# First down projection of a decoder layer in products of 512 columns, with the S5 setup cut in two and moved

## The chip, the cores and the metric

The kernel runs on one core of one Trainium2 chip. The metric is the device time of one execution in microseconds (us). Five engines work side by side, each through its own instructions in order: TensorE (PE, matrix products; its weight loads are listed as PEld), VectorE (DVE), ScalarE (ACT), GpSimd (POOL) and SyncE (SP, which here issues nearly all DMA transfers).

## The reference

One layer of a decoder trunk in float32, for 1024 tokens of width 1024 and a feed-forward width of 2816:

```
h = rms_norm(x, norm_w[0]);  x = x + 0.5 * (silu(h @ gate) * (h @ up)) @ down
h = rms_norm(x, norm_w[1]);  p = h @ w_in
y_A = S5(u)      lr = min(lam_re, -1e-4); dt = exp(log_dt); a = exp(lr*dt) * (cos(li*dt) + i sin(li*dt))
                 f = (a - 1)/(lr + i li);  Bb = f * B;  scan x_t = a x_{t-1} + Bb u_t;  y = Re(C x_t) + D u
y_B = HGRN2(q, f, v, g);   y_C = RG-LRU(conv(xb), gate)
x = x + (sum_b sigmoid(gate_b) * (y_b @ branch_proj_b)) @ w_out
h = rms_norm(x, norm_w[2]);  x = x + 0.5 * (second SwiGLU of h)
return rms_norm(x, final_norm_w)
```

S5 has 32 groups of 16 channels with 64 complex states each. What depends on its weights alone (powers of a, the products with B and C, a table of rotations) is computed in the kernel, and this setup is what the change moves.

## The kernel before

Every float32 operand of a product is split into two parts, high (h, a copy on ACT, L156 or L219) and low (l, the difference, on DVE, L157 or L220). A product of two split operands is three matmuls into the same PSUM bank (`mm3`, lines L207 to L209): wh with ah, wl with ah, wh with al. In the trace a matmul reads `ps<-w,ah`: first the moving operand with its columns, then the stationary one, a block of 128x128 that a weight load brings in ahead of it.

The first feed-forward has three stages. **Gate-up** (`gate_up`) makes the 22 blocks of silu(gate)*up by a scheme with seven products in place of eight (`tile7`). The **first down** (`down`, L526) multiplies blocks 0 to 9 of that result, the chunks CH1 = (4, 6), with the down weights. The other twelve blocks follow in `down7`, again by sevens. In `down` the results stand in four tiles X of 128 x 2 x 1024. A product covers 256 output columns (cq) and two row tiles (e) that share one PSUM bank of 512 columns, so that a matmul has 256 moving columns:

```
for e in range(2):
    t0 = (g % 2) * 256 + e * P
    ...
    self.mm3(ps[:, e * 256:(e + 1) * 256], pairs)
nc.vector.scalar_tensor_tensor(out=x, in0=ps.rearrange("p (e c) -> p e c", e=2), scalar=0.5, in1=x, op0=ALU.mult, op1=ALU.add)
next(hooks, None)
```

The last call but one (L558) is the evacuation: DVE adds half of the bank to x. Products of kind "g" have four banks, so the fifth product waits for the evacuation of the first. `next_units` hands out split weights from a ring of slots (RB = 3 raw tiles, HB = 6 halves); `a_split` loads and splits the blocks of the gate-up result (ar, ah, al).

`hooks` is the generator `s5_prep` (L1164): each product runs it to its next `yield`. It computes, in this order, the small values (tiles s5w, ex, An, half, tbc: 16 to 32 columns each, several hundred DVE instructions), Bb from B and those values, a table of rotations in four batches (tiles oc, os, otm; every other batch on POOL), and then eight batches of sums and turns. The sums of a batch are BA (two products and their sum) and Cn (the same, 576 columns). The second product of each, btm and t, runs on POOL, and DVE adds it. The turns are eight transposes on PE (L1372, ident or swap with BA), four products of Cn with Bb (L1383), and copies of their results.

A scheduler, not the order of the code, fixes each engine's order when the kernel is built: it places an instruction when its inputs should be there by its own costs, and `high_priority(PRIO)` moves splits ahead. On the chip each engine then keeps that fixed order.

Later, `s5_glu` and the merge of the three branches follow the mixers, and the second feed-forward ends with `down7` again, for which AL = 7 is the depth of the buffers `al`.

Of the kernel before, what the change touches and what calls it, by code (L numbers as in the profile page):

```python
# [12 lines left out]
P = 128  # L13
# [48 lines left out]
class Trunk:  # L62
    PRIO = 400
    RB, HB = 3, 6
# [188 lines left out]
    def x_in(self, g, cq):  # L253
        return self.I["x"][g * 256:(g + 1) * 256, cq * 256:(cq + 1) * 256].rearrange("(i p) c -> p i c", p=P)
# [93 lines left out]
    def ffn_units(self, n, chunks):  # L348
        g, u, dn = self.I["ffn_gate"][0, n], self.I["ffn_up"][0, n], self.I["ffn_down"][0, n]
        for f in range(NFF):  # L350
            self.add_cols(g, f * P, kind="n" if f < self.STD else "g")
            self.add_cols(u, f * P, kind=("n", "v")[f] if f < self.STD else "u")
        f0 = 0
        for c in chunks:
            step = c if c <= 4 else c // 2
            for cq in range(4):
                for f in range(f0, f0 + c, step):
                    self.add_cols(dn, cq * 256, f, step, 256)
            f0 += c
        self.d_units(n, f0 // 2)  # L360
# [141 lines left out]
    def a_load(self, upto, tag):  # L502
        while self.n_al < min(upto, len(self.aq)):
# [7 lines left out]
            self.nc.sync.dma_start(out=t, in_=self.abuf[f, hf])  # L511
# [14 lines left out]
    def down(self, chunks, x_src, hooks):  # L526
# [5 lines left out]
        for ci, c in enumerate(chunks):  # L532
            nu = 1 if c <= 4 else 2
# [4 lines left out]
            step = 2 if ci == 0 else 1  # L538
            for cq0 in range(0, 4, step):
                ws = {}  # L540
                for g, cq in ((2 * hf + i, cq0 + q) for hf in range(2) for q in range(step) for i in range(2)):
                    if cq not in ws:
                        ws[cq] = self.next_units(nu)
                    w = ws[cq]
                    x = self.X[g][:, :, cq * 256:(cq + 1) * 256]
# [3 lines left out]
                    for e in range(2):  # L549
                        t0 = (g % 2) * 256 + e * P  # L550
                        pairs = []
                        for k in range(c):
                            a = self.a[f0 + k, g // 2]
                            wt = w[k * nu // c]
                            kk = k % (c // nu)
                            pairs.append(((a[0][:, t0:t0 + P], a[1][:, t0:t0 + P]), (wt[0][:, kk, :], wt[1][:, kk, :])))
                        self.mm3(ps[:, e * 256:(e + 1) * 256], pairs)
                    nc.vector.scalar_tensor_tensor(out=x, in0=ps.rearrange("p (e c) -> p e c", e=2), scalar=0.5, in1=x, op0=ALU.mult, op1=ALU.add)  # L558
                    next(hooks, None)
                    if cq == 3 and g == 1 and ci > 0:  # L560
                        self.a_split(n1 + after)
                if cq0 + step == 4:
# [581 lines left out]
class S5(Mixer):  # L1144

    L = 8
# [4 lines left out]
    def s5_setup(self):  # L1151
        for _ in self.s5_prep():
            pass

# [9 lines left out]
    def s5_prep(self):  # L1164
        nc = self.nc
        V, A, G = nc.vector, nc.scalar, nc.gpsimd
        c = self.const
        NG, L, GB, NK = self.NG, self.L, self.GB, self.NK
        tt = lambda o, a, b, op, e=V: e.tensor_tensor(out=o, in0=a, in1=b, op=op)
        M, AD, SU = ALU.mult, ALU.add, ALU.subtract  # L1170
# [6 lines left out]

        self.rho = c.tile([P, NG], F32, name="rho")
        self.sc_w = [self.dram(n, (P, NG, P)) for n in ("s5w1a", "s5w1b", "s5ca1", "s5ca2")]
        self.sc_t = [self.dram(n, (P // 2, NG, NK)) for n in ("s5tc", "s5ts")]  # L1180
# [3 lines left out]
        swap = self.slot("p", (P, P), name="swap")  # L1184
        V.tensor_copy(swap[:, 0:64], self.ident[:, 64:128])
        V.tensor_copy(swap[:, 64:128], self.ident[:, 0:64])

        w = self.slot("p", (P, 16, NG), name="s5w")
        pr = self.slot("p", (P, 3, NG), name="s5p")
        self.get(pr, self.I["s5p"])  # L1190
        B1, B2, C1, C2 = (self.slot("p", (P, NG, 16), name=n) for n in ("B1", "B2", "C1", "C2"))
        for i, t in enumerate((B1, B2, C1, C2)):
            self.get(t, self.I["s5bc"][i])
        dsk = c.tile([16, NG], F32, name="dsk")
        self.get(dsk, self.I["s5d"])
        lr, dt, mag, th, n, cs, sn, den, f0, f1, t0, t1, fr, fi, e0, e1 = (w[:, i, :] for i in range(16))
        self.late = tsc(lr, pr[:, 0, :], -1e-4, ALU.min)
# [33 lines left out]
        tsc(fi, fi, sg, M)  # L1231

        An = [self.slot("p", (P, L + 1, NG), name=f"An{i}") for i in range(4)]
# [6 lines left out]
        tmp = self.slot("p", (P, L + 1, NG), name="tmp")  # L1240
        k = 1
        while k < L:
# [9 lines left out]
            k *= 2  # L1252
        tsc(sAr, Ar, sg, M)
# [6 lines left out]
        rv = self.slot("p", (P, 2, L, NG), name="rv")  # L1260
# [5 lines left out]
        Bb1, Bb2 = (self.slot("p", (P, NG, 16), name=n) for n in ("Bb1", "Bb2"))  # L1266
        tb = self.slot("p", (P, NG, 16), name="tb")
        frb, fib = (x.unsqueeze(2).to_broadcast([P, NG, 16]) for x in (fr, fi))
        tt(Bb1, B1, frb, M)
        tt(tb, B2, fib, M)  # L1270
        tt(Bb1, Bb1, tb, SU)
        tt(Bb2, B2, frb, M)
        tt(tb, B1, fib, M)
        tt(Bb2, Bb2, tb, AD)
        yield

        TB = 16
        HG = NG // 2
        tc_, ts_ = (self.slot("p", (P, HG, TB), name=n) for n in ("tbc", "tbs"))
# [20 lines left out]
        for _ in range(3):  # L1300
            square(er, ei, er, ei)
        er, ei, t0, t1 = (halved(t) for t in (er, ei, t0, t1))
# [3 lines left out]
        tmt = self.slot("p", (P, HG, TB // 2), name="tmt")  # L1306

        def double(oc, os, xc, xs, r, i, tm, gn, k, e=V):
            rb, ib = (x.unsqueeze(2).to_broadcast([P, gn, k]) for x in (r, i))
            tt(oc, xc, rb, M, e)  # L1310
            tt(tm, xs, ib, M, e)
            tt(oc, oc, tm, SU, e)
            tt(os, xc, ib, M, e)
            tt(tm, xs, rb, M, e)
            tt(os, os, tm, AD, e)
# [5 lines left out]
        mu = self.slot("p", (P, 6, HG), name="mu")  # L1321
        cur = (er, ei)
        for m in range(3):
            V.tensor_copy(mu[:, 2 * m, :], er)
            V.tensor_copy(mu[:, 2 * m + 1, :], ei)
            if m < 2:
                square(er, ei, er, ei)
        yield
# [17 lines left out]
        for b in range(nb):  # L1346
# [14 lines left out]
            flat = lambda t: t.rearrange("p g n c -> p g (n c)")  # L1361
# [6 lines left out]
            yield  # L1368
# [20 lines left out]
            self.put(self.sc_K[:, gs, :], kt)  # L1389
            yield  # L1390
# [86 lines left out]
class Hybrid(S5):  # L1477
# [166 lines left out]
    def ffn1(self):  # L1644
        nc = self.nc
        tiles = {}
        with ExitStack() as R:
            with ExitStack() as L:
# [25 lines left out]
                self.gate_up(0, lambda: self.t_first(normed(0, 2), 0, 2), lambda: self.t_second(normed(1), 0), self.CH1, {6: self.hg_masks, 9: self.hg_setup, 12: self.s5_zeros, 15: self.rg_setup}, 2)  # L1674
# [16 lines left out]
            self.w_open(self.H)  # L1691
# [126 lines left out]
```

## Time and profile before

| | us |
|---|---|
| median of 3 runs | 2298.42 (2298.32 to 2301.26) |
| the profiled execution, its own time | 2294.33 |
| its span, first to last instruction | 2292.1 |
| PE busy | 2238.5 |
| DVE busy | 1647.7 |
| ACT busy | 992.6 |
| POOL busy | 213.5 |

The span is 2.2 us shorter than that execution's own time, and the execution 4.1 us shorter than the median. Matmuls overlap in the pipeline, so the busy time of PE says where it had work, not how fast it went; the distance from one matmul's start to the next one's says that. A matmul that waits has in brackets how long PE stood idle before it and what is inferred to have released it.

### The profile page before, as it was taken

The page shows a single profiled execution, that of the slowest core. Times are in us where ns is not written, and L with a number is a line of the kernel's source. Part 1 is how long each engine was busy: PE and PEld are TensorE (multiplying, and loading weights), DVE is VectorE, ACT ScalarE, POOL GpSimd, SP SyncE. Part 2 cuts the span into 40 slices and gives each one's busy share as a digit, 9 for nine tenths or more (in the row PEclk, how much of TensorE's full clock was granted, in tenths as well). Part 3 has the DMA queues.
Part 4 walks back from the last instruction along what each step waited for, and adds up shares of the span by engine and source line. Part 5 has one row for each costly group of instructions (what it writes and reads, how often), then busy time and mean ns, then how long its engine had stood idle before and what let it go on. Part 6 is the DMA issues. An engine that isn't in the chain of part 4 may idle for free. (4 is left out here: it accounts for less than half of the span.)

```text
span 2292.1 us, 32136 instructions
## 1 busy us (share of the span) xinstructions
PE 2238.5 (98%) x11540; PEld 1889.0 (82%) x11540; DVE 1647.7 (72%) x2912; ACT 992.6 (43%) x1696; POOL 213.5 (9%) x218
## 2 busy tenths in 40 slices
PE   7999999999999999999999999999999999999998
PEld 6788888899789888888777788798978888888886
DVE  6876676699698765657777678867486766665797
ACT  5223222322457433435666666645432222234454
POOL 0200000004200300000000045610020000000000
PEclk9999999999999999999999999999999999999999
DMA  5122433474844465754343745356513433347633
GB/s 157 56 83 83 118 115 120 143 255 136 261 151 146 115 187 166 221 156 140 127 132 127 220 133 175 111 171 207 161 33 115 161 109 120 102 138 287 221 101 122
DMA packets 354367, 336.96 MB, mean 147 GB/s; under 512 B 44048, under 2 KB 258448, under 8 KB 354192
## 3 DMA queue, kind: packets, MB, share of 16 engines
q1 hardware_dynamic: 354208, 334.92, 46.4%
q8 instruction: 90, 1.47, 0.3%
q14 instruction: 69, 0.57, 0.1%
HBM read 233.53 MB, written 102.50 MB: 147 GB/s over the span
## 5 line engine op out<-in xcount | busy, mean ns | idle before, releaser
L207 PE MATMUL ps<-T,w 128*128 128x512 f32 (+1 forms) x992 | 380.7, 387 | 1.5 <-DVE T L309 1.2
L208 PE MATMUL ps<-T,w 128*128 128x512 f32 (+1 forms) x992 | 379.5, 384 | 1.3 <-DVE T L310 1.3
L209 PE MATMUL ps<-T,w 128*128 128x512 f32 (+1 forms) x992 | 376.3, 384 | 1.6 <-DVE w L157 1.6
L156 ACT CAST w<-raw 128x1024 fp32r<-128x1024 f32 (+2 forms) x218 | 182.2, 837 | 323.3 <-PE ps L208 290.6
L157 DVE TENSOR_TENSOR w<-raw,w 128x1024 fp32r<-128x1024 f32 (+2 forms) x218 | 216.7, 995 | 118.6 <-ACT w L156 113.6
L156 ACT CAST w<-S 128x1024 fp32r<-128x1024 f32 x128 | 134.5, 1051 | 337.1 <-PE ps L208 327.7
L208 PE MATMUL ps<-TT,w 128*128 128x512 f32 x640 | 252.3, 394 | 4.4 <-DVE TT L310 4.4
L207 PE MATMUL ps<-TT,w 128*128 128x512 f32 x640 | 250.6, 393 | 0.0
L209 PE MATMUL ps<-TT,w 128*128 128x512 f32 x640 | 249.6, 392 | 0.0
L209 PEld LDWEIGHTS ps<-T,w 128*128 128x128 f32 x992 | 187.3, 189 | 39.4 <-DVE w L157 3.1
L208 PEld LDWEIGHTS ps<-T,w 128*128 128x128 f32 x992 | 187.3, 189 | 38.5 <-DVE T L310 1.5
L207 PEld LDWEIGHTS ps<-T,w 128*128 128x128 f32 x992 | 186.4, 189 | 39.5 <-DVE T L309 1.9
L157 DVE TENSOR_TENSOR w<-S,w 128x1024 fp32r<-128x1024 f32 x128 | 158.7, 1240 | 73.3 <-ACT w L156 73.3
L411 DVE TENSOR_TENSOR g<-g,ps 128x512 f32<-128x512 f32 x132 | 90.2, 684 | 134.2 <-PE ps L209 125.7
L208 PEld LDWEIGHTS ps<-TT,w 128*128 128x128 f32 x640 | 120.8, 189 | 36.0 <-DVE TT L310 11.4
L207 PEld LDWEIGHTS ps<-TT,w 128*128 128x128 f32 x640 | 121.4, 190 | 25.7
L209 PEld LDWEIGHTS ps<-TT,w 128*128 128x128 f32 x640 | 121.1, 189 | 24.3
L156 ACT CAST ah<-ar 128x512 fp32r<-128x512 f32 (+2 forms) x153 | 80.2, 525 | 139.5 <-PE ps L208 89.4
L208 PE MATMUL ps<-b,ah 128*128 128x512 f32 x360 | 139.3, 389 | 0.0
L207 PE MATMUL ps<-b,ah 128*128 128x512 f32 x360 | 137.4, 389 | 0.0
L209 PE MATMUL ps<-b,ah 128*128 128x512 f32 x360 | 126.7, 390 | 0.0
L157 DVE TENSOR_TENSOR ah<-ar,ah 128x512 fp32r<-128x512 f32 (+2 forms) x153 | 85.8, 567 | 42.3 <-ACT ah L156 34.5
(414 smaller groups left out, 4884.3 us busy)
## 6 DMA issues: line engine op xcount, KB each, us to landing
raw<-in_w_in_dram SPq DMA_DIRECT2D x56, 512.0 KB
raw<-in_ffn_gate_dram SPq DMA_DIRECT2D x44, 512.0 KB
raw<-in_ffn_up_dram SPq DMA_DIRECT2D x44, 512.0 KB
B<-in_ffn_down_dram SPq DMA_DIRECT2D x68, 256.0 KB
ar<-s SPq DMA_DIRECT2D x68, 256.0 KB
ar<-a SPq DMA_DIRECT2D x66, 256.0 KB
s<-S SPq DMA_DIRECT2D x62, 256.0 KB
a<-a SPq DMA_DIRECT2D x56, 256.0 KB
```

What stands on the lines that cost most here:

```text
L156: self.nc.scalar.copy(hi, src)
L157: self.last_lo = self.nc.vector.tensor_tensor(out=lo, in0=src, in1=hi, op=ALU.subtract)
L207: nc.tensor.matmul(out=ps, lhsT=lh, rhs=rh, start=start and j == 0, stop=False, skip_group_check=skip)
L208: nc.tensor.matmul(out=ps, lhsT=lh, rhs=rl, start=False, stop=False, skip_group_check=skip)
L209: self.last_mm = nc.tensor.matmul(out=ps, lhsT=ll, rhs=rh, start=False, stop=stop and j == n - 1, skip_group_check=skip)
L411: tt = lambda o, a, b: nc.vector.tensor_tensor(out=o, in0=a, in1=b, op=ALU.add)
```

## The change

- **Products of 512 columns.** In `down` a product is now one row tile (q of 8) by one half of the columns, with one bank and one matmul of 512 columns per step. Weights come in units of two blocks by 512 columns, seven slots of halves (HB = 7), and x comes in sixteen loads of 128x512, issued behind the eighth load of the gate-up result.
- **Small values in gate-up.** `s5_small` is a generator of its own, run one step per gate-up block from f = 3, with its tiles in a pool of its own.
- **The rest of the setup, sums a batch ahead.** `s5_prep` starts with B and C, then Bb, the table and the sums of batch 0; after that the sums of batch b + 1 are issued before the turns of batch b.
- **Pools.** 13 slots p and 4 slots pc instead of 14 and 3; `w_open` moves to the next pool; the last down has 6 buffers al.

```
-    RB, HB = 3, 6
+    RB, HB = 3, 7
...
-            step = c if c <= 4 else c // 2
-            for cq in range(4):
-                for f in range(f0, f0 + c, step):
-                    self.add_cols(dn, cq * 256, f, step, 256)
+            for half in range(2):
+                for f in range(f0, f0 + c, 2):
+                    self.add_cols(dn, half * HALF, f, 2, HALF)
...
             if ci == 0:
+                self.a_split(2 * c)
+                first_a = self.a_ins
                 self.a_split(2 * c + sum(chunks[1:2]))
...
+            for half in range(2):
+                w = self.next_units(c // 2)
+                for q in range(8):
+                    x = self.X[q // 2][:, q % 2, half * HALF:(half + 1) * HALF]
                     if ci == 0:
-                        nc.sync.dma_start(out=x, in_=x_src(g, cq))
+                        with self.tc.issue_after(first_a.ins):
+                            nc.sync.dma_start(out=x, in_=x_src(q, half))
                     ps = self.ps("g")
...
+                    c0 = slice((q % 4) * P, (q % 4 + 1) * P)
+                    pairs = []
+                    for k in range(c):
+                        a, wt = self.a[f0 + k, q // 4], w[k // 2]
+                        pairs.append(((a[0][:, c0], a[1][:, c0]), (wt[0][:, k % 2], wt[1][:, k % 2])))
+                    self.mm3(ps, pairs)
+                    nc.vector.scalar_tensor_tensor(out=x, in0=ps, scalar=0.5, in1=x, op0=ALU.mult, op1=ALU.add)
                     next(hooks, None)
...
-        for b in range(nb):
+        def sums(b):
...
-            yield
+            return BA, Cn
+
+        def turned(b, BA, Cn):
+            gs = slice(b * GB, (b + 1) * GB)
             for q, idm in enumerate((self.ident, swap)):
...
+        last = sums(0)
+        yield
+        for b in range(nb):
+            new = sums(b + 1) if b + 1 < nb else None
+            yield
+            turned(b, *last)
+            last = new
             yield
...
+                small = self.s5_small()
+                midway = {f: lambda: next(small, None) for f in range(3, NFF)}
+                midway.update({6: self.hg_masks, 9: self.hg_setup, 12: self.s5_zeros, 15: self.rg_setup})
+                self.gate_up(0, lambda: self.t_first(normed(0, 2), 0, 2), lambda: self.t_second(normed(1), 0), self.CH1, midway, 2)
...
+            for _ in small:
+                pass
             with ExitStack() as c:
                 self.open_pool(c, a=24)
-                self.open_pool(c, "left", p=14, pt=6, pc=3)
+                self.open_pool(c, "left", p=13, pt=6, pc=4)
                 self.down(self.CH1, self.x_in, self.prep())
...
-            self.open_pool(R, al=7, X=4, fw=1)
+            self.AL = 6
+            self.open_pool(R, al=6, X=4, fw=1)
```

**DVE where the first down begins.** `al` are low parts of the gate-up result, `x<-ps` the evacuation of the first product, `ex` and `s5w` small values of S5. Before, the evacuation stands behind a run of `al` with two small instructions between each pair:

```order
586 L220 TENSOR_TENSOR al_3913<-ar_3900,ah_3912 128x512
587 L800 TENSOR_SCALAR ex_4062<-ex_4063 128x32
588 L1176 SCALAR_TENSOR_TENSOR s5w_4019<-s5w_4019 128x32
589 L220 TENSOR_TENSOR al_3919<-ar_3902,ah_3918 128x512
590 L802 SCALAR_TENSOR_TENSOR ex_4063<-ex_4062,ex_4063 128x32
591 L1176 SCALAR_TENSOR_TENSOR s5w_4019<-s5w_4019 128x32
592 L220 TENSOR_TENSOR al_3925<-ar_3904,ah_3924 128x512
593 L558 SCALAR_TENSOR_TENSOR x_3888<-ps_3953,x_3888 128x2x256
```

Now, in the same place (`Cn`, `Bb` and `BA` are the wide sums of the S5 batches, `oc`, `os` and `otm` the rotation table, `t` a product that POOL makes):

```order
798 L1158 TENSOR_TENSOR Cn_4605<-C_746_4285,s5An_1954 128x576
799 L220 TENSOR_TENSOR al_4181<-ar_4178,ah_4180 128x512
800 L220 TENSOR_TENSOR al_4191<-ar_4184,ah_4190 128x512
801 L1158 TENSOR_TENSOR Bb_749_4294<-Bb_749_4294,tb_4295 128x512
802 L220 TENSOR_TENSOR al_4195<-ar_4186,ah_4194 128x512
803 L1158 TENSOR_TENSOR otm_4319<-os_4318,s5mu 128x4x32
804 L1158 TENSOR_TENSOR oc_4317<-oc_4317,s5mu 128x4x64
805 L1158 TENSOR_TENSOR os_4318<-oc_4317,s5mu 128x4x64
806 L220 TENSOR_TENSOR al_4199<-ar_4188,ah_4198 128x512
807 L1158 TENSOR_TENSOR Cn_4605<-Cn_4605,t_797_4606 128x576
808 L220 TENSOR_TENSOR al_4205<-ar_4202,ah_4204 128x512
809 L552 SCALAR_TENSOR_TENSOR x_4174<-ps_4245,x_4174 128x512
```

Between the last instruction of gate-up (`u_4102`, row 780) and the evacuation (row 809) there now stand 28 instructions: 12 of 512 columns, 6 of 576 (the third, fourth and last of which add a `t`), and 10 table steps (3 of 64 columns, 5 of 128, 2 of 256).

**POOL in the same place.** Its first instructions of the S5 setup, up to the product t_797 that DVE's row 807 adds, are rows 21 to 37: six table steps of 64 columns, six of 128, two of 256, and three products t. The last nine of them:

```order
29 L1158 TENSOR_TENSOR t_771_4491<-C_747_4286,s5An_1955 128x576
30 L1158 TENSOR_TENSOR t_777_4521<-C_747_4286,s5An_1955 128x576
31 L1158 TENSOR_TENSOR otm_4361<-os_4360,s5mu 128x4x32
32 L1158 TENSOR_TENSOR oc_4359<-oc_4359,otm_4361 128x4x32
33 L1158 TENSOR_TENSOR otm_4361<-os_4360,s5mu 128x4x32
34 L1158 TENSOR_TENSOR oc_4359<-oc_4359,s5mu 128x4x64
35 L1158 TENSOR_TENSOR os_4360<-oc_4359,s5mu 128x4x64
36 L1158 TENSOR_TENSOR os_4360<-os_4360,otm_4361 128x4x32
37 L1158 TENSOR_TENSOR t_797_4606<-C_747_4286,s5An_1955 128x576
```

Before, POOL's first S5 instruction was a `t` whose sum stood far behind the first evacuations.

**SP ahead of the merge of the branches.** `raw<-in_s_glu_w` loads weights of `s5_glu`; v, f, k, q and g are inputs of the HGRN2 mixer. Before, two such loads stand behind all of these:

```order
655 L819 DMA v_12385<-v_7354 128x512
656 L819 DMA f_12394<-pf_0_7975 128x512
657 L819 DMA k_12396<-pk_0_7983 128x512
658 L819 DMA q_12398<-pq_0_7991 128x512
659 L819 DMA g_12400<-pg_0_7999 128x512
660 L819 DMA f_12633<-pf_0_7977 128x512
661 L819 DMA k_12635<-pk_0_7985 128x512
662 L819 DMA q_12637<-pq_0_7993 128x512
663 L819 DMA g_12639<-pg_0_8001 128x512
664 L144 DMA raw_12215<-in_s_glu_w_dram 128x4x128
665 L144 DMA raw_12242<-in_s_glu_w_dram 128x4x128
```

Now the first stands among the v and the second behind the first f:

```order
647 L813 DMA v_11894<-v_6859 128x512
648 L144 DMA raw_11727<-in_s_glu_w_dram 128x4x128
649 L810 DMA p_7_0_7549<-u_11564 128x512
650 L813 DMA v_11895<-v_6860 128x512
651 L813 DMA v_11896<-v_6861 128x512
652 L813 DMA v_11897<-v_6862 128x512
653 L813 DMA f_11906<-pf_0_7487 128x512
654 L144 DMA raw_11754<-in_s_glu_w_dram 128x4x128
```

So those two weight loads have moved ahead of 11 and of 7 of the mixer's loads in SP's queue.

## Rows read from the trace of the kernel before

**Rows 1.** The page: each engine's busy time, share of the span and instructions.
```profile
PE 2238.5 (98%) x11540; PEld 1889.0 (82%) x11540; DVE 1647.7 (72%) x2912; ACT 992.6 (43%) x1696; POOL 213.5 (9%) x218
```

**Rows 2.** PE's waits: line, releaser, us in total, times, longest.
```profile
PE ps L1372 <- DVE BA L1169: 5.0, 2, 4.0
...
PE ps L207 <- ACT w L156: 3.0, 1, 3.0
...
PE ps L208 <- DVE w L157: 1.9, 2, 1.0
```

**Rows 3.** By window: busy us and instructions per engine, granted clock, DMA share, GB/s.
```profile
300.00:400.00 100.00, 100.00 (x443) 82.81 (x442) 72.52 (x142) 29.18 (x38) 0.52 (x1) 1.00 0.37 119
...
480.00:490.00 10.00, 10.00 (x87) 10.00 (x86) 9.66 (x35) 3.33 (x6) 0.00 (x0) 1.00 1.07 361
...
580.00:585.00 5.00, 2.10 (x10) 1.74 (x11) 4.17 (x7) 0.67 (x2) 1.53 (x1) 0.72 0.89 258
585.00:590.00 5.00, 5.00 (x27) 4.27 (x26) 2.26 (x4) 1.78 (x4) 2.29 (x2) 0.60 0.35 118
...
1305.00:1310.00 5.00, 4.12 (x11) 3.17 (x12) 2.11 (x4) 2.49 (x4) 0.00 (x0) 0.66 0.48 137
```

**Rows 4.** PE from 456 to 593 us by shape: count, busy us, mean ns, idle before.
```profile
L208 PE MATMUL ps<-w,ah 128*128 128x256 f32 x320 | 90.3, 284 | 1.0 <-DVE w L157 1.0
```

**Rows 5.** PE, start and us of each, at the first down's fifth product.
```profile
470.34 0.28 PE L208 MATMUL ps<-w,ah 128*128 128x256 f32 x1
470.46 0.28 PE L209 MATMUL ps<-w,al 128*128 128x256 f32 x1
472.44 0.36 PE L207 MATMUL ps<-w,ah 128*128 128x256 f32 x1 [1.71 <-DVE ex L802]
```

**Rows 6.** DVE, start and us of each, from the end of gate-up.
```profile
460.89 0.69 DVE L455 TENSOR_TENSOR u<-g,u 128x512 f32<-128x512 f32 x1 [0.49 <-ACT g L450]
461.50 0.17 DVE L798 TENSOR_SCALAR ex<-s5p 128x32 f32<-128x32 f32 x1
...
471.01 0.68 DVE L220 TENSOR_TENSOR al<-ar,ah 128x512 fp32r<-128x512 f32 x1
471.61 0.68 DVE L558 SCALAR_TENSOR_TENSOR x<-ps,x 128x512 f32<-128x512 f32 x1
```

**Rows 7.** DVE at two moments at which POOL works too.
```profile
547.00 1.27 DVE L1173 TENSOR_SCALAR half<-half 128x16 f32<-128x16 f32 x2
...
579.32 1.26 DVE L1169 TENSOR_TENSOR Cn<-Cn,t 128x576 f32<-128x576 f32 x1 [4.89 <-POOL t L1169]
```

**Rows 8.** POOL around the same moments, by size.
```profile
544.01 0.29 POOL L1169 TENSOR_TENSOR otm<-os,mu 128x64 f32<-128x64 f32 x1
...
546.48 0.44 POOL L1169 TENSOR_TENSOR os<-oc,mu 128x128 f32<-128x128 f32 x1
546.89 1.27 POOL L1169 TENSOR_TENSOR t<-C,An 128x576 f32<-128x576 f32 x1
...
574.32 0.61 POOL L1169 TENSOR_TENSOR oc<-oc,mu 128x256 f32<-128x256 f32 x1
...
579.24 0.72 POOL L1169 TENSOR_TENSOR os<-os,otm 128x256 f32<-128x256 f32 x1
```

**Rows 9.** All executions of one DVE form: ns least, median and most.
```profile
L1169 DVE TENSOR_TENSOR Cn<-Cn,t x8: 733/750/1648, 507.3 to 607.3; 128x576 f32<-128x576 f32 x8
```

**Rows 10.** PE in the start stage and at the merge.
```profile
32.33 0.39 PE L208 MATMUL ps<-T,w 128*128 128x256 f32 x1 [1.30 <-DVE T L310]
...
1305.88 0.79 PE L207 MATMUL ps<-zsh,w 128*128 128x512 f32 x1 [2.98 <-ACT w L156]
```

**Rows 11.** SP's queue ahead of the merge: start and us of the issues.
```profile
1294.36 0.32 SPq L819 DMA_DIRECT2D f<-pf  x1
...
1299.54 1.06 SPq L144 DMA_DIRECT2D raw<-in_s_glu_w_dram  x2
```

More of the change, by code (lines that the diff above doesn't have):

```diff
@@ L537, in down @@
             after = sum(chunks[ci + 1:ci + 2])
[L538 to L545, printed above, removed]
+            for half in range(2):
+                w = self.next_units(c // 2)
+                for q in range(8):
+                    x = self.X[q // 2][:, q % 2, half * HALF:(half + 1) * HALF]
                     if ci == 0:
-                        nc.sync.dma_start(out=x, in_=x_src(g, cq))
+                        with self.tc.issue_after(first_a.ins):
+                            nc.sync.dma_start(out=x, in_=x_src(q, half))
                     ps = self.ps("g")
[L549 to L558, printed above, removed]
+                    c0 = slice((q % 4) * P, (q % 4 + 1) * P)
[5 more added lines that the diff above has]
+                    nc.vector.scalar_tensor_tensor(out=x, in0=ps, scalar=0.5, in1=x, op0=ALU.mult, op1=ALU.add)
                     next(hooks, None)
-                    if cq == 3 and g == 1 and ci > 0:
+                    if half == 1 and q == 3 and ci > 0:
                         self.a_split(n1 + after)
-                if cq0 + step == 4:
+                if half == 1:
                     self.a_split(n1 + 2 * after)
@@ L1162, in s5_zeros, with s5_ops, tt @@
             self.put(self.sc_T[16 * s:16 * s + 16, :, 0:16 * s], zr[0:16, 0:16 * s].unsqueeze(1).to_broadcast([16, self.NG, 16 * s]))
[L1164 to L1170, printed above, removed]
+    def s5_ops(self):
+        V = self.nc.vector
+        def tt(o, a, b, op, e=V):
+            return e.tensor_tensor(out=o, in0=a, in1=b, op=op)
         def tsc(o, a, s1, op0, s2=None, op1=None):
@@ L1176, in stt, with double, s5_small @@
             V.scalar_tensor_tensor(out=o, in0=a, scalar=s, in1=b, op0=op0, op1=op1)
+        def double(oc, os, xc, xs, r, i, tm, gn, k, e=V):
+            rb, ib = (x.unsqueeze(2).to_broadcast([P, gn, k]) for x in (r, i))
+            tt(oc, xc, rb, ALU.mult, e)
+            tt(tm, xs, ib, ALU.mult, e)
+            tt(oc, oc, tm, ALU.subtract, e)
+            tt(os, xc, ib, ALU.mult, e)
+            tt(tm, xs, rb, ALU.mult, e)
+            tt(os, os, tm, ALU.add, e)
+        return tt, tsc, stt, double
+    def s5_small(self):
+        nc = self.nc
+        V, A = nc.vector, nc.scalar
+        c = self.const
+        NG, L = self.NG, self.L
+        tt, tsc, stt, double = self.s5_ops()
+        M, AD, SU = ALU.mult, ALU.add, ALU.subtract
+        zt = lambda shape, name, tag=None: self.Zp.tile(list(shape), F32, name=name, tag=tag or name, bufs=1)
         self.rho = c.tile([P, NG], F32, name="rho")
-        self.sc_w = [self.dram(n, (P, NG, P)) for n in ("s5w1a", "s5w1b", "s5ca1", "s5ca2")]
-        self.sc_t = [self.dram(n, (P // 2, NG, NK)) for n in ("s5tc", "s5ts")]
         sg = c.tile([P, 1], F32, name="sgn")
@@ L1183, in s5_prep @@
         V.memset(sg[64:128], -1.0)
[L1184 to L1189, printed above, removed]
-        self.get(pr, self.I["s5p"])
[L1191 to L1195, printed above, removed]
+        w = zt((P, 16, NG), "s5w")
+        pr = zt((P, 3, NG), "s5p")
+        self.get(pr, self.I["s5p"])
         lr, dt, mag, th, n, cs, sn, den, f0, f1, t0, t1, fr, fi, e0, e1 = (w[:, i, :] for i in range(16))
-        self.late = tsc(lr, pr[:, 0, :], -1e-4, ALU.min)
+        self.order(tsc(lr, pr[:, 0, :], -1e-4, ALU.min), self.last_lo)
         li = pr[:, 1, :]
@@ L1231, in s5_prep @@
         tsc(fi, fi, sg, M)
-        An = [self.slot("p", (P, L + 1, NG), name=f"An{i}") for i in range(4)]
+        yield
+        An = [zt((P, L + 1, NG), f"s5An{i}") for i in range(4)]
         Ar, nsAi, sAr, nAi = An
@@ L1252, in s5_prep @@
             k *= 2
+        yield
         tsc(sAr, Ar, sg, M)
@@ L1305, in s5_prep @@
         mults = []
[L1306 to L1315, printed above, removed]
+        tmt = zt((P, HG, TB // 2), "s5tmt")
         k = 1
```

69 lines of the change are left out of this document (45 added, 24 removed).

## The prediction

> **What bounds the kernel now.** I read the page first: PE is busy for 98% of the span [rows 1], so the kernel is PE's work plus the few places where PE waits or runs at its lower clock. Next the waits of PE, where the reader is to see which of them the change touches: 5.0 us in two waits of the S5 transposes for BA, 3.0 us in one wait for a weight part on ACT, and one of 1.0 us for a weight part on DVE [rows 2]. Then windows, to see which engine fills its time. In gate-up, PE and nothing else is full: 443 matmuls in 100 us, so 0.2257 us from one 512-column matmul to the next, with PEld at 83% and DVE at 73%. In the first down PEld is full as well (10.00 of 10), with 87 matmuls in 10 us, which is 0.115 us for 256 columns, and DVE is at 97% [rows 3]. So the first down is where three engines are full at once, and what stands in DVE's order there decides what PE gets. Last the timeline of PE and DVE at the start of that stage: PE's fifth product needs the bank of the first, and stood idle for 1.71 us until DVE had evacuated it. The releaser named there is a small instruction, but the evacuation from 471.61 to 472.29 is the one that ends just before PE starts at 472.44 [rows 5, 6].
>
> **The sum**, against the profiled execution of 2294.33 us; as the median is 4.1 us above it, I add the same sum to 2298.42.
>
> *Columns: -3.0.* 960 matmuls of 256 columns go, a third of them in one row [rows 4], and 480 of 512 come. 480 x 0.2257 = 108.3 us. The old ones took 960 x 0.115 = 110.4 by the window, or 960 x 0.12 = 115.2 by the distance of two neighbours [rows 3, 5]. The gain is between 2.1 and 6.9; I take 3.0, near the window, which counts many. The Trainium skill, TensorE: Matmul & The Clock Gate, section Back-to-back issue gap, gives an isolated matmul about N / 2.4 + 2.5 ns, that is 109 and 216 ns; by that the gain would be an estimated 1.2 us. The trace's distances are longer at both sizes, and they decide.
>
> *The wait at the fifth product: +12.3.* Before, DVE's small instructions filled the time until the al could be made. They are gone to gate-up, and the scheduler has put the wide S5 sums in their place, in front of the evacuation: 28 instructions between the end of gate-up (461.50, rows 6) and the evacuation, which is the 29th. A 512-column one takes 0.60 us from its start to the next one's [rows 6], 13 of them with the evacuation are 7.8. Six of 576 at 0.67 (the median of 0.75 less the 0.08 by which neighbours overlap, rows 6, 9) are 4.0. Ten table steps of 64 to 256 columns, scaled from 0.60 by their width with 0.07 fixed, are 2.2. Sum 14.0, so the evacuation cannot be done before 475.5. PE is through with its four products at about 470.0 (470.58 by rows 5, less what four products of 512 columns save). Lower end of the wait: 5.6.
>
> The upper end comes from POOL. DVE's last Cn ahead of the evacuation adds t_797, and ahead of that POOL has 17 instructions: three t at 1.27, six of 64 columns at 0.29, six of 128 at 0.44, two of 256 at 0.61, together 9.4 us [rows 8]. Beside DVE they would be hidden. But they do not run beside it: two 16-column instructions of DVE took 1.27 us, exactly while a t of 1.27 ran on POOL, and a Cn that takes 0.75 otherwise took 1.26 while a table step of POOL had the first 0.6 of it [rows 7 to 9]. If no two of these overlap, the evacuation is done at 461.5 + 14.0 + 9.4 = 484.9 and PE waits 14.9. I take 14.0, close to the upper end, because both rows show full exclusion; the first steps of POOL fall into DVE's gaps. Against 1.71 before: +12.3. The Trainium skill, SBUF — State Buffer, section Who interferes with whom, says that a DVE instruction with two SBUF inputs and a GpSimd instruction that reads SBUF block each other for the whole instruction. By it the wait is 14.9, without it 5.6; the rows stand with it. Queued behind this evacuation are those of the next three banks and the al of blocks 5 to 9, which are not needed for another dozen products.
>
> *Waits that go: -6.0.* The two waits for BA (5.0) and the 1.0 for a weight part [rows 2]. The sums now stand a batch ahead of their transposes.
>
> *What is late next: +4.0.* The same DVE and POOL still have most of the eight batches, the rest of the table and the weight splits to do while PE wants its banks and transposes. All may go (0) or as much return as went (6.0). I take 4.0, nearer to the upper end, for POOL and DVE exclude each other here too.
>
> *Clock: +1.0.* After the 4.0 us wait the granted clock was 0.72 and 0.60 in two windows of 5 us [rows 3]: half of the 2.1 busy us of the first, and 0.4 x 5 of the second, 3.0 us in all. That goes. A wait of 14 us will bring at least the same, and a second dip may follow a later wait: 4.0. Ends: -3.0 and +3.0.
>
> *Start stage: +1.2.* Some exponentials of S5, thirteen instructions of 32 columns at 0.1 to 0.17, are placed among the splits T on which PE waits already for 1.30 us [rows 6, 10]. 13 x 0.1 = 1.3 if all are on the path, 0 if none, and up to 2.5 if their input lands late; I take 1.2.
>
> *Small values in gate-up: 0.* DVE has 27 us free in each 100 us there [rows 3], and PE has no wait in that window. They are several hundred at 0.1 us, some 35 us in 300. If bunches of them hold up an evacuation: up to +4.
>
> *Merge: -3.0.* One weight load of s5_glu was issued at 1299.54 behind all of the mixer's loads, 5 us after the first f at 1294.36 [rows 11], and PE waited 2.98 for it and then ran at clock 0.66 for 5 us, 1.7 us lost [rows 3, 10]. Both loads now stand 7 to 11 places further ahead. At most 4.7 comes back; I take 3.0, since what is queued behind may be late in turn. x behind the gate-up result, and the pools: 0, because DVE's order, not a landing, holds PE at the fifth product, and no wait of the last down stands among PE's longer ones [rows 2]; at most 2 either way.
>
> Sum: -3.0 + 12.3 - 6.0 + 4.0 + 1.0 + 1.2 - 3.0 = +6.5, so 2304.9 us.
>
> **The rivals.**
> 1. *DVE and POOL do overlap* at the start of the first down. For it: the DVE window from 480 is 97% full with PE never waiting, but POOL was idle there [rows 3], so this says little; against it rows 7 and 8. The wait is then 5.6 (+3.9 for 12.3), nothing returns later (0 for 4.0) and one dip replaces one (0 for 1.0): -3.0 + 3.9 - 6.0 + 1.2 - 3.0 = -6.9, 2291.5. It turns faster than before by more than 0.2% once the wait is under 7.9 with nothing late after it.
> 2. *The merge does not gain*: DMA is full there, and an earlier issue lands no sooner. Then +9.5, 2307.9. For it: of the time to PE's start at 1305.88, 6.3 us lie behind the issue [rows 10, 11], and what shares the queue is the same; against it, an issue some 4 us earlier has fewer bytes ahead of it.
> 3. *Gate-up is held up* by bunches of small values: +4 on the forecast, 2308.9. Against it, the same instructions stood in the first down beside a full PE with no wait at 480 [rows 3].
> 4. *The fifth product does not wait longer than before*, because the order's place does not matter: then the change does what it is said to do. -3.0 + 0 - 6.0 + 0 - 3.0 + 1.2 - 3.0 = -13.8, 2284.6. Against it: an in-order engine and a bank that only the evacuation frees.
>
> **How the numbers follow.** Forecast 0.55, rival 1 0.12, rival 2 0.20, rival 3 0.08, rival 4 0.05. The forecast's own range is 2300 to 2309 (wait 12 to 15, late next 2 to 6). The range that holds 8 in 10 leaves out rival 4 and half of rival 1 below, and rivals 2 and 3 together with a second dip above: 2290 to 2312. A measurement of this kernel can tell 0.2%, 4.6 us, from no change: slower is above 2303.0. Of the forecast about 0.7 lies above that, with rivals 2 and 3: 0.66. Faster is rivals 1 and 4 with nearly all of their chance: 0.16. The rest, 0.18, is the same.
>
> **What the changed profile would show.** Right: PE's longest wait of the first down at its fifth product, near 470 us, of 12 to 15 us, and a granted clock of half after it; in it DVE's Cn and table steps with durations 0.3 to 1 us above their medians, POOL busy beside them; the waits of L1372's transposes for BA gone or under 3 us each; 480 matmuls at 0.226. Wrong: a wait under 8 us there, DVE's Cn at 0.75 while POOL is busy, or waits of PE in gate-up between 100 and 450 us. The wait of 2.98 us at the merge tells rival 2 from the forecast.

## The result and the profile after

The changed kernel takes 2312.01 us (median; 2311.31 to 2313.01) against 2298.37 for the kernel before on the same chip: a ratio of 1.0063, 95% interval 1.0049 to 1.0077. It is slower by 13.6 us; 2304.9 was predicted, in a range up to 2312. The profiled executions, 2294.33 and 2313.01 us, lie 18.7 us apart, because that of before was a short one; the landmarks below are of these two.

The page of the profile after, beside [rows 1], has 480 matmuls fewer, and PE is still the bound:

```profile
PE 2235.9 (97%) x11060; PEld 1866.5 (81%) x11060; DVE 1645.5 (71%) x2910; ACT 991.1 (43%) x1694; POOL 220.9 (10%) x218
```

Two starts on PE's timeline cut the execution into three parts. These are the first matmul of the first down and the first of the stage behind it, in before:

```profile
456.32 0.28 PE L207 MATMUL ps<-w,ah 128*128 128x256 f32 x1
...
615.29 0.50 PE L207 MATMUL ps<-b,ah 128*128 128x512 f32 x1
```

and the same two in after:

```profile
462.82 0.39 PE L207 MATMUL ps<-w,ah 128*128 128x512 f32 x1
...
631.54 0.50 PE L207 MATMUL ps<-b,ah 128*128 128x512 f32 x1 [1.44 <-ACT u L674]
```

So up to the first down after has lost 6.5 us, in the first down (159.0 us before, 168.7 now) 9.7, and behind it (spans of 2292.1 and 2311.2) 2.9; these are the 19.1 us by which the two spans differ. The longest waits of PE in after, beside [rows 2], are:

```profile
PE ps L207 <- DVE x L552: 16.1, 1, 16.1
...
PE ps L207 <- DVE u L410: 9.4, 5, 3.9
PE ps L207 <- DVE th L1604: 3.3, 2, 2.7
```

The transposes' waits for BA and the merge's 3.0 us for w have gone from the head of the list. In their place stand one wait of 16.1 us for an evacuation, five for `u` and two for `th`. The windows of after show what each does to the clock (columns as in [rows 3]):

```profile
270.00:280.00 10.00, 6.06 (x20) 4.51 (x20) 5.24 (x8) 2.05 (x3) 0.00 (x0) 0.74 0.37 104
280.00:285.00 5.00, 5.00 (x20) 4.05 (x19) 3.04 (x4) 2.71 (x3) 0.00 (x0) 0.84 0.28 91
470.00:480.00 10.00, 6.58 (x30) 5.11 (x28) 10.00 (x14) 3.68 (x6) 9.27 (x12) 0.98 1.01 359
480.00:490.00 10.00, 0.00 (x0) 0.00 (x0) 10.00 (x12) 1.25 (x2) 8.26 (x7) 0.50 0.41 131
490.00:500.00 10.00, 7.27 (x24) 5.81 (x25) 10.00 (x22) 2.47 (x4) 0.00 (x0) 0.67 0.78 215
```

**The fifth product.** PE ends its fourth product at 476.58 and starts the fifth at 492.73, at the lower of its clock's two levels (granted 0.50 in the window, 1.2 of 2.4 GHz; columns of [rows 5]):

```profile
476.19 0.39 PE L209 MATMUL ps<-w,al 128*128 128x512 f32 x1
492.73 0.76 PE L207 MATMUL ps<-w,ah 128*128 128x512 f32 x1 [16.14 <-DVE x L552]
```

On DVE these are the last instruction of gate-up, two of the S5 steps behind it, and the evacuation (a row with x2 holds two instructions):

```profile
467.84 0.68 DVE L454 TENSOR_TENSOR u<-g,u 128x512 f32<-128x512 f32 x1
...
470.35 0.50 DVE L1158 TENSOR_TENSOR oc<-oc,s5mu 128x128 f32<-128x128 f32 x1
...
472.31 1.31 DVE L1158 TENSOR_TENSOR os<-oc,s5mu 128x128 f32<-128x128 f32 x1
...
491.91 1.27 DVE L552 SCALAR_TENSOR_TENSOR x<-ps,x 128x512 f32<-128x512 f32 x2
```

The first step of 128 columns takes 0.50 us, the second 1.31. Beside the second POOL is in two t, which take 2.90 us together where [rows 8] have 1.27 for one:

```profile
471.80 2.90 POOL L1158 TENSOR_TENSOR t<-C,s5An 128x576 f32<-128x576 f32 x2
```

From the end of gate-up's last `u` (468.52) to the end of the first evacuation (492.54, half of the row's x2) are 24.0 us; the prediction had 14.0 + 9.4 = 23.4. Of the 24.0, DVE was idle for 0.74, for the load of B.

**Gate-up.** PE waits 3.94 us for `u`, in a stretch in which the prediction had no cost:

```profile
276.42 0.80 PE L207 MATMUL ps<-T,w 128*128 128x512 f32 x1 [3.94 <-DVE u L410]
```

DVE stood idle for 10.77 us ahead of it, for a weight load:

```profile
261.64 1.22 DVE L157 TENSOR_TENSOR w<-raw,w 128x1024 fp32r<-128x1024 f32 x1
273.62 0.69 DVE L177 TENSOR_TENSOR S<-raw 128x512 f32<-128x512 f32 x1 [10.77 <-DMA raw<-in_ffn_up_dram]
...
274.96 0.68 DVE L410 TENSOR_TENSOR u<-g,ps 128x512 f32<-128x512 f32 x1
```

The sum S of weight blocks needs the load, and `u`, whose bank PE wants, stands behind S. SP's queue tells why the load is late; in after it is issued at 267.48, behind seven transfers that write the zeros of s5T:

```profile
255.38 9.57 SPq L810 DMA_DIRECT2D s5T<-zr  x7
...
267.48 2.12 SPq L144 DMA_DIRECT2D raw<-in_ffn_up_dram  x1
```

In before the same load was issued ahead of them:

```profile
254.85 0.38 SPq L144 DMA_DIRECT2D raw<-in_ffn_up_dram  x1
256.57 8.46 SPq L816 DMA_DIRECT2D s5T<-zr  x7
```

**The merge.** The wait of 2.98 us [rows 10] is now two of 0.69 and 0.82, but one for `th` follows:

```profile
1322.67 0.50 PE L207 MATMUL ps<-zsh,w 128*128 128x512 f32 x1 [0.69 <-ACT w L156]
1324.23 0.50 PE L209 MATMUL ps<-zsh,w 128*128 128x512 f32 x1 [0.82 <-DVE w L157]
1334.97 0.50 PE L207 MATMUL ps<-yh,w 128*128 128x512 f32 x1 [2.72 <-DVE th L1604]
```

### The profile page after: what moved, and what is told of

Its sections match the earlier page's. It is cut to its first block, busy times and chain, and to the rows that moved or that the text cites. A ratio compares the mean times of both kernels' runs of the same rounds, so it can differ in the third digit from the quotient of the medians.

```text
span 2311.2 us, 31004 instructions
## 1 busy us (share of the span) xinstructions
PE 2235.9 (97%) x11060; PEld 1866.5 (81%) x11060; DVE 1645.5 (71%) x2910; ACT 991.1 (43%) x1694; POOL 220.9 (10%) x218
## 5 line engine op out<-in xcount | busy, mean ns | idle before, releaser
L156 ACT CAST w<-raw 128x1024 fp32r<-128x1024 f32 (+1 forms) x216 | 181.9, 842 | 295.1 <-PE ps L209 189.5
L157 DVE TENSOR_TENSOR w<-raw,w 128x1024 fp32r<-128x1024 f32 (+1 forms) x216 | 212.7, 986 | 59.0 <-PE ps L208 45.0
L207 PE MATMUL ps<-h,w 128*128 128x512 f32 x288 | 113.9, 396 | 5.5 <-DVE u L410 5.5
```

The source lines that it names most:

```text
L156: self.nc.scalar.copy(hi, src)
L157: self.last_lo = self.nc.vector.tensor_tensor(out=lo, in0=src, in1=hi, op=ALU.subtract)
L207: nc.tensor.matmul(out=ps, lhsT=lh, rhs=rh, start=start and j == 0, stop=False, skip_group_check=skip)
```

## The experiments

"Against before" is the difference of the medians on the same chip in the same session. After is at +13.6. The intervals of these ratios are 0.1 to 0.2% to either side, 2 to 4 us, and where two runs are compared both apply.

**1. POOL's S5 products on DVE.**

```
-        V, A, G = nc.vector, nc.scalar, nc.gpsimd      (in s5_prep of after)
+        V, A, G = nc.vector, nc.scalar, nc.vector
```

> The changed kernel, with every product of the S5 setup that POOL made (t, btm, every other table batch) made by DVE instead. DVE thereby gets more work ahead of the first evacuation. Theory A (DVE and POOL exclude each other, so POOL's time stands in DVE's way): a 576-column product costs DVE 0.67 us where POOL's blocked it for some 1.2, so the wait at the fifth product falls from 16.1 to 6 to 10 us, the later waits of the first down go, and the kernel is 8 to 13 us faster than the changed one (2299 to 2304). Rival B (the two run side by side, the wait is DVE's own instructions): the wait grows by the work that is added, to 18 to 21 us, and the kernel is 2 to 5 us slower (2314 to 2317).

Measured: 2301.92 us, ratio 1.0017 (1.0006 to 1.0028), +4.4 against before. The wait for the evacuation, in this kernel's waits:

```profile
PE ps L207 <- DVE x L552: 7.2, 1, 7.2
```

DVE got all of POOL's work and was done earlier. Here two engines were slower than one.

**2. The S5 setup behind the fourth evacuation.**

```
-                    nc.vector.scalar_tensor_tensor(out=x, in0=ps, ...)
-                    next(hooks, None)
+                    ev = nc.vector.scalar_tensor_tensor(out=x, in0=ps, ...)
+                    seen += 1
+                    if seen == 4:
+                        gate = ev
+                    if seen >= 4:
+                        with self.tc.issue_after(gate.ins):
+                            next(hooks, None)
```

> The changed kernel, with every S5 instruction of DVE in the first down ordered behind the evacuation of the fourth product. Theory A (DVE's order made the 16.1 us): the wait at the fifth product falls under 2 us; the sums, beside POOL, now collide with later evacuations and transposes, and 5 to 12 us of waits come back between 490 and 560 us; net 3 to 9 us faster than the changed kernel (2303 to 2309). Rival C (x, or the gate-up result, lands late, and the order is no cause): a wait of 10 us or more stays at the fifth product, and the time is within 2 us of 2312.

Measured: 2305.01 us, ratio 1.0034 (1.0022 to 1.0047), +7.5. The waits of this kernel:

```profile
PE ps L1395 <- DVE BA L1163: 4.1, 1, 4.1
PE ps L207 <- DVE x L552: 4.0, 2, 3.0
```

With POOL still at work, about half of the 16 us is still waited for: 1.0 at the fifth product, and 7.1 later, for BA and one more evacuation.

**3. The zeros of s5T behind the loads already issued.**

```
+        with self.tc.issue_after(self.raw_ins[self.n_raw - 1].ins):
             for s in range(1, self.L):
                 self.put(self.sc_T[...], zr...)
```

> The changed kernel, with the seven zero transfers of S5 in gate-up issued behind the next up and gate weights in SP's queue, as the up weights were before the change. Theory A (the 3.94 us wait near 276 us came from that queue): the wait and the stretch at the lower clock behind it go, 6 to 7 us faster than the changed kernel (2305 to 2306). Rival D (the small values on DVE in gate-up held the up weights' sums): the wait stays, within 1 us of 2312.

Measured: 2309.08 us, ratio 1.0051 (1.0033 to 1.0069), +11.6, so 2.0 better than after where 6 to 7 were expected. The wait at 276 us went, but the seven transfers now stood ahead of the next load, and PE waited 2.18 us at 293.64, again for `u`.

So an `up` load stands behind the seven again. In before a `gate` load does (issued at 267.44), and there PE does not wait: in these runs the seven cost time only ahead of an `up` load, whose sum S stands ahead of `u` on DVE.

**4. Pairs of instructions on DVE and POOL by themselves** (the layer is left out; the output holds only what keeps the instructions alive).

```
for i in range(10): DVE.tensor_tensor(da, da, a)       # alone, then POOL alone (pa)
DVE: db = db*a, POOL: pb = pb*b                        # together, 576 columns
DVE: ds = ds*c (16 columns, one input), POOL: pc       # together
DVE: dx = ps*c + dx (ps in PSUM), POOL: pd             # together
```

> A small program of its own, which leaves out all of the layer and only copies x: products of 576 columns on DVE alone, on POOL alone, on both at once; then 16-column instructions of one input on DVE beside POOL; then DVE instructions with one input in PSUM alone and beside POOL. Theory A (exclusion for the whole instruction): alone 0.67 us from start to start on DVE and 1.2 on POOL; at once the two take turns, so that DVE's go up to some 1.8 each while POOL works, or POOL's do; the 16-column ones wait up to 1.2; those with an input in PSUM are not slowed. Rival B (side by side): all the same as alone, within 10%.

Measured, by shape (count, busy us, mean ns of one):

```profile
L84 DVE TENSOR_TENSOR db<-db,a 128x576 f32<-128x576 f32 x22 | 25.6, 1237 | 0.0
L84 POOL TENSOR_TENSOR pb<-pb,b 128x576 f32<-128x576 f32 x8 | 15.0, 1907 | 0.0
L113 DVE SCALAR_TENSOR_TENSOR dx<-ps,dx 128x512 f32<-128x512 f32 x24 | 14.7, 682 | 0.0
L84 POOL TENSOR_TENSOR pd<-pd,b 128x576 f32<-128x576 f32 x6 | 8.2, 1402 | 0.0
L84 POOL TENSOR_TENSOR pa<-pa,b 128x576 f32<-128x576 f32 x6 | 8.2, 1398 | 0.0
...
L84 DVE TENSOR_TENSOR da<-da,a 128x576 f32<-128x576 f32 x10 | 6.8, 755 | 0.0
...
L102 DVE TENSOR_SCALAR ds<-k 128x16 f32<-128x16 f32 x4 | 2.8, 773 | 0.0
```

Alone, 576 columns take 755 ns on DVE and 1398 on POOL; together they take turns (1907 on POOL; the 22 of DVE mix those beside POOL with those behind its end). So a pair takes 1.9 us in turns, where two on DVE alone take 1.5. The 16-column instruction with one input, 773 ns beside POOL, is held up as well. One that reads PSUM and one SBUF input is not (682 ns, and 1402 for POOL beside it). The Trainium skill, SBUF — State Buffer, section Who interferes with whom, says the same: two SBUF inputs on DVE against a GpSimd instruction that reads SBUF exclude each other, at most one SBUF input outside its two-port modes does not. By that an evacuation does not itself lose time to POOL; it waits for the S5 instructions ahead of it, which do.

**5. The zeros spread over seven blocks of gate-up.**

```
+          with self.tc.issue_after(self.raw_ins[self.n_raw - 1].ins):
             self.put(self.sc_T[...], zr...)
+          yield
...
+  midway.update({f: lambda: (next(zeros, None), next(small, None)) for f in (7, 8, 10, 11, 12, 13, 14)})
```

> The kernel after, with the seven zero transfers of s5T issued one at a time in seven blocks of gate-up, each behind the weight loads already issued (the zeros come from a tile in the pool of the small values). Theory A: the wait near 276 us and the half clock behind it come only from a weight load that stands behind all seven zero transfers in SP's queue (about 8.5 us of issues); with one transfer (1.2 to 1.4 us) between two loads nothing is late. PE has no wait over 1 us between 100 and 450 us, and the kernel is 6 to 7 us faster than after: 2305 to 2306. The 16 us wait at the fifth product of the first down stays. Rival B: the small values on DVE are what makes gate-up tight, and the wait comes back at another block: at least 2 us of waits between 250 and 450, and 2308 to 2312.

Measured: 2304.6 us, ratio 1.0032 (1.0021 to 1.0044), +6.4, and no wait of PE over 0.25 us between 100 and 450 us. All small values are still in gate-up here, so they cost nothing there.

**6. The edits of 1, 2 and 5 together.**

> The kernel after with three edits: POOL's S5 products on DVE, the S5 setup held behind the fourth evacuation of the first down, and the zeros of s5T spread as in the run before. Theory A (three separate causes: POOL keeps DVE out, the order of DVE ahead of the first evacuation, and SP's queue): no wait over 3 us between 100 and 600 us, so the waits of 16.1 and 3.9 us, their half clocks and nothing in their place: 16 to 22 us less than after, 2290 to 2296, so faster than before by 0.1 to 0.4%. Rival B: DVE simply has too much to do in the first down, and what is held back is waited for later: waits of 5 us or more between 500 and 620, and 2298 to 2303.

Measured: 2287.92 us, ratio 0.9964 (0.9951 to 0.9976), -10.3. Against after the single edits gave 9.2, 6.1 and 7.2 us, 22.5 in all, and together 23.9. PE's longest wait between 100 and 600 us is 1.8 us, so rival B falls. The time is below theory A's range too. That the gains add up fits three causes, but the intervals are wide, and the edits of 1 and 2 act on the same wait.

**7. The kernel before with the 512-column products alone** (`down`, `x_in`, the weight units and x behind a as in after; S5 and the six slots as in before).

> The kernel before with one part of the change alone: the first down in products of 512 columns (weight halves of two rows of blocks, x by blocks of 128 rows and 512 columns, issued behind a); S5's setup, POOL and the six slots stay as before. The prediction's term for the columns is -3.0 (ends -2.1 and -6.9), and the waits for BA stay: 2293 to 2296. Rival: PE was limited there by DVE's evacuations and splits, whose number and size do not change, and the columns give nothing: 2297 to 2299, with new waits of PE for evacuations or weight parts between 460 and 610 us.

Measured: 2289.31 us, ratio 0.9964 (0.9952 to 0.9976), -8.9: more than either theory expected. The first down in this kernel:

```profile
456.41 0.39 PE L207 MATMUL ps<-w,ah 128*128 128x512 f32 x1
...
607.30 0.50 PE L207 MATMUL ps<-b,ah 128*128 128x512 f32 x1
```

150.9 us instead of 159.0. Waits there are 2.7 + 2.4 where before had 1.7 + 0.9 + 1.0 + 4.0, which is 2.6 less; 5.5 us are left for the columns.

**8. The kernel before with POOL's products on DVE** (the edit of 1, made in before).

> The kernel before with POOL's S5 products on DVE, nothing else. Theory A (a two-input instruction of POOL keeps DVE out for its whole time): moving them costs DVE no time, since each held it longer on POOL (1.27 us for 576 columns) than it takes on DVE (0.67): at most the order changes, 2295 to 2301. Rival B (they ran side by side): DVE, at 97% in the windows of that stage, gets some 15 to 20 us more to do, and the kernel is 5 us or more slower: 2303 to 2312.

Measured: 2299.79 us, ratio 1.0013 (1.0005 to 1.0022), +1.6. DVE takes the products almost for nothing, but they gain nothing here either. In the profiled execution the first down is 13.7 us shorter (145.3) and what follows 19.4 longer (1696.2 against 1676.8): the last batches come later, and PE waits for them there.

```profile
PE ps L1372 <- DVE dg L1169: 6.7, 1, 6.7
PE ps L1372 <- DVE BA L1169: 4.5, 1, 4.5
```

**9. The kernel before with its zeros where after has them** (the edit of 3, made in before: there it puts the seven between a gate load and the next up load).

> The kernel before, with only the place of the seven s5T zero transfers in SP's queue changed: they now stand behind the gate weights of the tenth block and ahead of the next up weights, the place they have in after; DVE's small values stay where they were in before. Theory A (the gate-up wait is the queue's and not the small values'): a wait of 2 to 5 us for u near 276 to 295 us with a granted clock of about half behind it, and 3 to 7 us more than before: 2301 to 2305. Rival B (only together with the small values on DVE does a late load cost anything): no wait over 1 us in gate-up and the time of before, 2297 to 2299.

Measured: 2304.09 us, ratio 1.0027 (1.0017 to 1.0038), +7.1. SP and DVE of this kernel:

```profile
268.07 8.00 SPq L816 DMA_DIRECT2D s5T<-zr  x6
...
281.06 0.81 SPq L144 DMA_DIRECT2D raw<-in_ffn_up_dram  x1
```
```profile
287.71 0.69 DVE L177 TENSOR_TENSOR S<-raw 128x512 f32<-128x512 f32 x1 [9.78 <-DMA raw<-in_ffn_up_dram]
288.32 0.68 DVE L411 TENSOR_TENSOR u<-g,ps 128x512 f32<-128x512 f32 x1
```

PE waits for that `u`:

```profile
290.25 0.80 PE L207 MATMUL ps<-T,w 128*128 128x512 f32 x1 [4.98 <-DVE u L411]
```

Without a single small value in gate-up, the queue alone costs what after lost there.

**10. The three edits with six slots of weight halves.**

```
-    RB, HB = 3, 7
+    RB, HB = 3, 6
```

> The kernel of the three edits (POOL's products on DVE, S5 behind the fourth evacuation, zeros spread) with six slots of weight halves in place of seven. Theory A (the seventh slot only moves the wait at the merge from a weight part to th, and is worth nothing): the time of the three edits, 2286 to 2290, with the wait of 2.7 us for th or one of about 3 us for a weight part near 1300 to 1311 us. Rival B (the seventh slot carries part of the gain, by earlier splits): 2292 to 2297, with new waits of PE for w in the first down or at the merge.

Measured: 2279.33 us, ratio 0.9917 (0.9899 to 0.9935), -17.6. Neither theory: the seventh slot is not worth nothing, it costs 7.3 us by the medians (3.0 by the two profiled executions, 2285.54 and 2282.57). The first down is the same (151.4 us with seven, 151.6 with six); the gain is behind it. This is the fastest version, and it beats both kernels.

**11. After with six slots, nothing else** (the edit of 10).

> The kernel after, with six slots of weight halves in place of seven, nothing else. The run with three edits and six slots had a median 8.6 us below that with seven, most of it behind the first down. Theory A (the seventh slot lets the scheduler put a weight sum or split on DVE ahead of an evacuation although its load has not landed, DVE sits idle for the load and PE for the bank): the waits for u near 1125 us (2 us) and for th near 1335 us (2.7 us) go or shrink below 1.5, and the kernel is 3 to 9 us faster than after: 2303 to 2309, with the 16 us wait and the gate-up wait as they were. Rival B (the two medians differ for another reason, such as the chip or the session): 2310 to 2313 with the later waits unchanged.

Measured: 2298.98 us, ratio 1.0012 (1.0001 to 1.0024), +3.0, so 10.6 us better than after; 3 to 9 were expected. I had the gate-up wait stay, and it went:

```profile
257.63 0.38 SPq L144 DMA_DIRECT2D raw<-in_ffn_up_dram  x1
258.77 8.79 SPq L810 DMA_DIRECT2D s5T<-zr  x7
```

With six slots the load is issued ahead of the zeros again, as in before. The waits of this kernel keep the long one and lose those for `u` but for 1.9 us, as much as before has:

```profile
PE ps L207 <- DVE x L552: 15.6, 1, 15.6
...
PE ps L207 <- DVE u L410: 1.9, 2, 1.3
```

Of the four later waits for `u` in after, two (0.65 and 1.38) have counterparts in before. At the longest, 2.31 us at 1132.70, DVE's order in after is:

```profile
1129.91 0.69 DVE L177 TENSOR_TENSOR S<-raw 128x512 f32<-128x512 f32 x1 [1.47 <-DMA raw<-in_w_in_dram]
...
1131.24 0.68 DVE L410 TENSOR_TENSOR u<-g,ps 128x512 f32<-128x512 f32 x1
```

A weight sum stands ahead of an evacuation and waits for a load that has not landed, as at 276. The other waits that go with six slots do not show this form. At 1279.51 (`u`, 1.17) and 792.99 (T, 2.01) DVE is busy without a pause, and at 1334.97 (`th`, 2.72) two scans stand in front. What they have in common is only that they go with the slot. Behind the first down, the profiled executions of the six whole kernels with S5's new order and seven slots take 1675.1 to 1679.7 us, those of the three with six slots 1667.1 to 1672.0. How the scheduler comes to these orders isn't shown.

**12. The kernel of 10 with POOL's products back on POOL.**

> The kernel of the three edits with six slots, but POOL keeps its S5 products: S5 behind the fourth evacuation, zeros spread, six slots. Theory A (turn-taking of DVE and POOL costs wherever both have wide work): waits of 3 to 8 us in all for evacuations or BA between 490 and 600 us, and 4 to 9 us more than with the products on DVE: 2283 to 2289. Rival B (it cost only because it stood ahead of the first evacuation): no wait over 2 us there and the time of the three edits, 2277 to 2281.

Measured: 2289.33 us, ratio 0.9966 (0.9953 to 0.9979), -6.6, so 11.0 more than the kernel of 10. Its waits:

```profile
PE ps L1397 <- DVE BA L1165: 3.7, 1, 3.7
PE ps L207 <- DVE x L552: 3.2, 2, 2.6
```

The first down takes 158.7 us (455.82 to 614.48) against 151.6. So POOL's share costs 7.1 us there even with the first evacuations out of its way. What it costs the whole kernel stays open, between 0.8 and 11.0: the profiled execution, 2283.40, is the shortest of its five (the others 2287.9 to 2289.8) and only 0.8 us above that of run 10, because it reaches the first down 1.4 us sooner and is 4.9 us shorter behind it (1667.1 against 1672.0).

## Why the prediction was too low

The sign and the main mechanism were right, the size was half: 6.5 forecast, 13.6 measured.

**The step that failed is the seventh slot of weight halves, which the sum has at nothing.** It has no term of its own. At most it falls under "the pools: 0 ... at most 2 either way", and the reasons given there, DVE's order at the fifth product and the waits of the last down, say nothing of weight slots. Taken back, the slot gives 10.6 us (run 11). By the profiled executions of after and run 11, which lie 17.0 us apart, 5.6 of these are ahead of the first down (the weight load behind the zeros in SP's queue), 2.8 in it and 8.6 behind it, where PE waits less for `u` (3.6 in all), T (2.0), ACT's `u` (1.4) and `th` (1.7). One of those later waits is shown to come from a load that had not landed; what moved the others is open. Nothing in the trace of before has a seventh slot, so the term needed two ends.

**"Small values in gate-up: 0 ... up to +4"** is where 6.5 of the loss appears, and its cause was put wrong in the rival too. A wait of PE there was one of the prediction's own signs of being wrong. The small values cost nothing: in after their last is done at 195 us, 80 us ahead of the wait, and with them still in gate-up run 5 reaches the first down at 456.35 us, before at 456.32. The seven transfers did cost, at 1.2 to 1.4 us of issue each, once they stood ahead of an `up` load (run 9: +7.1 in before). The prediction counted what a load is moved past in SP's queue at the merge, but not here.

**"The wait at the fifth product: +12.3"** had the right mechanism: at its upper end 23.4 us of DVE and POOL in turns, 24.0 measured. The size was short: 16.1 against 1.7 before is +14.4. The wait is above the upper end, 14.9, by those 0.6, because PE ended its fourth product 8.1 us behind DVE's end of gate-up where the forecast had 8.5, and by 0.2 from the evacuation's end to PE's start. Rival 1 falls with runs 1 and 4, rival 4 with the wait itself.

**"Columns: -3.0"** was small, if run 7 is taken whole: its first down loses 5.5 us beyond its waits. Half clocks do not explain that, as by the prediction's way of counting both kernels lose about 3 us to them. Where PE is full in both (480 to 540 us), before has 514 matmuls and run 7 has 265; at 0.1167 and 0.2264 us each that makes 3.4 us for the stage, close to the forecast. The other 2.1 are not located.

**"Waits that go" and "late next"**: BA's 5.0 us went as forecast. In after only 1.3 us came back in the rest of that stage, not 4.0. Why is not shown: of the eight batches only the first BA starts before PE does at 492.73 (they run from 480.6 to 554.6). Where S5 stands behind the fourth evacuation and POOL still works (runs 2 and 12), 7.1 and 6.3 us came back.

**"Clock: +1.0"**: behind the 16 us wait the clock is 0.67 over 7.3 busy us, 2.4 us, where before lost 3.0 behind BA's. The dip in gate-up, 0.74 and 0.84, came on top and belongs to the term that failed.

**"Merge: -3.0"** did not show in after: the wait for w shrank by 1.5, but `th` waits 2.7 instead of 0.7, and a clock of 0.66 now stands behind that (1335 to 1340 us). With six slots (run 11) it did: 1.2 us for w, 1.6 for `th` and a clock of 1.00 from 1300 to 1330, some 2.7 us less than before lost there. The longest wait for `th` is 2.7 to 2.9 us in all six kernels with seven slots and the new order, and 1.2 to 1.6 in the three with six. So it was the slot, and not rival 2, that took the gain. **"Start stage: +1.2"** did not show, by the same two starts of the first down, 456.35 and 456.32.

What the parts are worth, against before: the products of 512 columns with their loads of x -8.9 (run 7); the seventh slot +10.6 (after less run 11); all the rest of the change, which is S5's new order with POOL beside it and the pools, +11.9 (run 11 less run 7). They make up the 13.6 because the last is a difference; the pools were not tried by themselves.

## What to carry to other kernels

One buffer more is not a free edit where a scheduler sets the order of in-order engines: it can move other work in front of what PE waits for. Look in the order for instructions that wait for a DMA and now stand in front of an evacuation, and for loads that now stand behind other transfers in their queue. Several small-row transfers in one queue should be spread, or put where the next load behind them is not needed soon. If DVE and POOL both read two SBUF operands, sharing the work between them saves no time; ahead of something that PE waits for it belongs on one of them, and the first evacuations of a stage belong ahead of it.

## What the runs showed of the chip

Sharing wide two-input work between DVE and POOL made it slower than DVE alone where PE waited for it: 9.2 us in after (run 1), and 7.1 us of the first down in the best version (run 12). In before, moving it to DVE gained nothing (run 8: +1.6). An instruction of DVE with one small SBUF input is held up as well, 773 ns for 16 columns where one of 32 took 170 [rows 6], while one that reads PSUM and one SBUF operand runs at 682 ns beside POOL and does not slow it (run 4). A transfer of 512 rows of 64 to 448 bytes holds SP's queue for 1.2 to 1.4 us, 8.5 to 9.6 us for seven, and DVE stood idle for 7.0 to 10.8 us for an `up` load issued behind seven of them (runs 3 and 9, and after).
